# Part of the adaLN modulation of a two-block transformer: matmuls per k-tile replaced by VectorE sums and one matmul over the partitions

## The chip, the cores and the metric

The kernel runs on one core of one Trainium2 chip. The engines of a core are TensorE (PE in the profile, PEld for its weight loads), VectorE (DVE), ScalarE (ACT), GpSimd (POOL) and SyncE (SP, which here issues DMAs). The metric is the time of one execution in microseconds of the device; lower is better.

## What is computed

Two blocks in a row act on 256 tokens of width 1024 (`x`) and on 256 context tokens (`ctx`). All arrays are fp32. The change lies in the first block, which has two layers, each a half feed-forward, an attention mixer, and another half feed-forward; every one of these is wrapped in a modulated norm and a gated residual. The modulation of layer i is a matrix-vector product:

```python
def adaln(cond, w, b):
    m = jax.nn.silu(cond) @ w + b
    return m.reshape(m.shape[:-1] + (N_MOD, D_MODEL))   # 9 x 1024

def modulated_norm(h, g, m, k):
    return rmsnorm(h, g) * (1.0 + m[..., k + 1, :]) + m[..., k, :]

def gated_residual(h, y, g, m, k, weight):
    return h + weight * m[..., k + 2, :] * rmsnorm(y, g)

# layer i:   m = adaln(c, ada_w[i], ada_b[i]);  mc = adaln(c_ctx, ada_w[i], ada_b[i])
#   half_ffn with m rows 0, 1, 2;  mixer with rows 3, 4, 5;  half_ffn with rows 6, 7, 8
```

`ada_w[i]` is 1024 x 9216 (37.7 MB), and there are only two conditions, `c` and `c_ctx`. The feed-forward is `(silu(gate) * up) @ w_out` with 2816 inner columns. The second block (a hybrid layer, twice) is not touched.

## The kernel before

Activations are kept transposed, features on the partitions and the 512 tokens (256 and 256) along the free axis, as eight tiles of 128 features. Every large product is done with three matmuls (`mm3`, lines 78 to 80): weights and activations are each split into a high and a low part, and high x high, low x high and high x low are added up in PSUM. The split of a weight tile is a cast on ScalarE (`wh`, line 60) and a subtraction on VectorE (`wl`, line 61), out of `raw` tiles which SP loads (line 52, three buffers); there are four buffers each of `wh` and `wl`.

A feed-forward (`ffn`) goes through 22 pairs of gate and up columns in three passes of 6, 8 and 8. In each iteration it prepares four weight tiles, runs 24 matmuls for each, takes silu of the gate on ScalarE (line 317), multiplies by up on VectorE (line 319) and splits the product (lines 323 and 324); after each pass `wout` multiplies by the output weights. PSUM gives four banks to gate and up.

The modulation is computed as filler. `ada_w[i]` is cut into 18 blocks of 512 columns, and these into groups of four blocks (`groups`). `adaln` returns a list of functions for a group: loads of 128x512 tiles `adaw` (line 156), eight steps, and a finish. A step takes the four tiles of one k-tile and multiplies each by the 32 columns of `cst` that begin with the two conditions of that k-tile; the four matmuls lie side by side in column strips of the array (line 164), and eight steps add up in one PSUM bank `psada`. The finish copies the bank (line 170), transposes it in four matmuls (line 175) and adds the bias into `mT` (line 182). `set_fill` takes such a list and a number of places; `place`, called after each column pair of `ffn`, each output pair of `wout` and twice in each quarter of an attention head, runs as many functions as keep the list evenly spread. A feed-forward has 22 + 8 = 30 places, the attention `da` 64. A scheduler behind the program orders each engine's instructions by the order of the program and its own estimate of when they can start; on the chip each engine then takes its queue in that order.

Group (i, g) is computed here: (0, 0) before the first feed-forward; (0, 1) and (0, 2) in the first feed-forward, whose `Join` at the end needs them; (0, 3), (1, 0) and (1, 1) in `da`; (0, 4), (1, 2) and (1, 3) partly in steep stretches between stages and partly in the next feed-forward; (1, 4) in the second attention. The small buffers are shared by tags: `adaw` has eight (tag W), and the tag P (four buffers) holds the probabilities of attention and the sums at a feed-forward's end.

Of the kernel before, what the change touches and what calls it, by code (L numbers as in the profile page):

```python
# [6 lines left out]
AF = mybir.ActivationFunctionType  # L7
ALU = mybir.AluOpType
# [4 lines left out]
KC = 8  # L13
# [12 lines left out]
SBUF_TAGS = ({"y": 10, "t": 4, "P": 4, "W": 8},  # L26
             {"d": 10, "e": 7, "m": 7, "t": 1, "th": 2, "E": 3, "br": 4, "mg": 3, "z": 2})
SBUF_OF = {}
for _t, _n in (("y", "y q qh ql kh kl v"), ("W", "adaw sAB sC gPT"), ("t", "q0 k0 sg g adasb vT trot osq o ksq qsq lr lp vr crow csil"), ("P", "P0 P1 PT P aAB aC"),
               ("d", "kz iq kR sc csq ck dq kd vd dPT ya"), ("e", "sbq sbk sbv sbvt yb"), ("m", "mlu mlth mlv wt hn yc"),  # L30
               ("th", "th tho uk"), ("E", "rl dE"), ("br", "bh bl"), ("mg", "mg"), ("z", "z")):
    SBUF_OF.update({n: _t for n in _n.split()})
# [11 lines left out]
class Block:  # L44
# [5 lines left out]
    def load(self, src, nk, cols):  # L50
        raw = self.rawp.tile([128, 8, 256], F32, name="raw", tag="raw")
        self.nc.sync.dma_start(raw[:, 0:nk, 0:cols], src.rearrange("(k p) c -> p k c", p=128))
        return raw
# [87 lines left out]
    def adaln(self, i, blocks, tiles="adaw", ahead=2):  # L141

        nc = self.nc
        nj, b0 = len(blocks), blocks[0]
        gap = blocks[1] - b0
        nm = 4 // nj
        steps = KC // nm
        st = {}

        def load(n):  # L150
            st[n] = []
            for k in range(n * nm, n * nm + nm):
                src = self.I['ada_w'][i, k * 128:(k + 1) * 128, :].rearrange("p (b c) -> p b c", c=512)
                for j in range(nj):
                    w = self.sp.tile([128, 512], F32, name="adas", tag="slot") if tiles == "slot" else self.t2("adaw")
                    nc.sync.dma_start(w, src[:, b0 + gap * j, :])
                    st[n].append(w)

        def step(n):
            if n == 0:  # L160
                st['ps'] = self.pst("psada")
            for q, w in enumerate(st[n]):
                k = n * nm + q // nj
                mm = nc.tensor.matmul(st['ps'][32 * q:32 * q + 32, :], lhsT=self.cst[:, 2 * k:2 * k + 32], rhs=w,
                                      start=n == 0, stop=n == steps - 1, tile_position=(0, 32 * q))
                self.tc.keep_in_program_order(mm)

        def take():
            st['sb'] = self.t2("adasb")
            nc.vector.tensor_copy(st['sb'], st['ps'])  # L170

        def finish():
            pt = self.pst("psadt")
            for q in range(4):
                nc.tensor.transpose(pt[:, q * 128:(q + 1) * 128], st['sb'][:, q * 128:(q + 1) * 128], self.ident)
            g = gap * (nj - 1) + 1
            dst = self.mT[i][:, b0 * 4:(b0 + g) * 4, :].rearrange("p (g q) r -> p q g r", q=4)[:, :, 0:g:gap, :]
            b = self.adab[:, 72 * i + b0 * 4:72 * i + (b0 + g) * 4].rearrange("p (g q) -> p q g", q=4)[:, :, 0:g:gap]
            b = b.unsqueeze(3).to_broadcast([128, 4, nj, 2])
            src = pt.rearrange("p (q m j r) -> p m q j r", q=4, m=nm, r=32)  # L180
            for m in range(nm):
                nc.vector.tensor_tensor(dst, src[:, m, :, :, 0:2], dst if m else b, ALU.add)

        def part(n):
            if n >= 0:
                step(n)
            for k in range(ahead) if n < 0 else (n + ahead,):
                if k < steps:
                    load(k)

        return [lambda n=n: part(n) for n in range(-1, steps - 1)] + [lambda: (step(steps - 1), take()), finish]

    def gtab(self, i, kind, k, out=None, cs=slice(0, 8)):

        nc = self.nc
        t = self.gp.tile([128, 8, 2], F32, name="gt", tag="gt") if out is None else out
        if kind == 'pre':
            j, gi, add, mul = k + 1, {0: 0, 3: 2, 6: 4}[k], 1.0, 1.0
        else:
            j, gi, add, mul = k + 2, {0: 1, 3: 3, 6: 5}[k], 0.0, (1.0 if k == 3 else 0.5)  # L200
        g0, n = (i * 6 + gi) * 8, cs.stop - cs.start
        g = self.ng[:, g0 + cs.start:g0 + cs.stop].unsqueeze(2).to_broadcast([128, n, 2])
        nc.vector.tensor_scalar(t[:, cs, :], self.mT[i][:, j * 8 + cs.start:j * 8 + cs.stop, :], add, mul, ALU.add, ALU.mult)
        nc.vector.tensor_tensor(t[:, cs, :], t[:, cs, :], g, ALU.mult)
        return t
# [1083 lines left out]
    def first_block(self):  # L1289
        nc, I, both = self.nc, self.I, (0, 1)  # L1290
        groups = [range(4 * g, min(4 * g + 4, 18)) for g in range(5)]
        fill = lambda *gs: sum([self.adaln(i, groups[g], ahead=1) for i, g in gs], [])

        us, steps = [], self.adaln(0, (0, 2), "slot", 4)
        us.extend(self.ffn_units(0, 0, 0))

        def begin():
            steps.pop(0)()
            return steps

        R = self.load_tokens(begin)
        for f in steps:
            f()
        self.new_x()
        G = self.gp.tile([128, 8, 2], F32, name="gt", tag="gt")

        def part(cs):
            self.gtab(0, 'pre', 0, G, cs)
            for c in range(cs.start, cs.stop):
                for hf in both:  # L1310
                    s, B = HALF[hf], self.mT[0][:, c, hf:hf + 1]
                    t = self.tp.tile([128, 256], F32, name="t", tag="t", bufs=4)
                    nc.vector.scalar_tensor_tensor(t, self.h[hf][c], G[:, c, hf:hf + 1], R[:, s], ALU.mult, ALU.mult)
                    nc.scalar.activation(self.xh[c][:, s], t, AF.Identity, bias=B)  # L1314
                    if hf:
                        self.low(self.xl[c][:, s], t, B, self.xh[c][:, s])
                    else:
                        nc.vector.scalar_tensor_tensor(self.xl[c][:, s], t, B, self.xh[c][:, s].bitcast(F32), ALU.add, ALU.subtract)

        def steep(i, g):  # L1320

            fl = fill((i, g))
            self.ramp = fl[0:4]
            return fl[4:]

        mid = [us] + self.adaln(0, (1, 3), "slot", 4) + [lambda: part(slice(4, 8))]
        part(slice(0, 4))
        self.ffn(0, 0, both, Join(self, (0, 0), (0, 3)), fill((0, 1), (0, 2)), AF.Exp, mid)
        self.dumph('h1_0')
        self.set_fill(fill((0, 3), (1, 0), (1, 1)), 64)  # L1330
        rest = steep(0, 4)
        self.da(Join(self, (0, 3), (0, 6)))
        self.dump('ya_0', self.y)
        last, rest = rest, steep(1, 2)
        self.ffn(0, 1, both, Join(self, (0, 6), (1, 0)), last)
        self.dumph('h3_0')
        last, rest = rest, steep(1, 3)
        self.ffn(1, 0, both, Join(self, (1, 0), (1, 3)), last, AF.Exp)
        self.set_fill(rest, 10)
        self.edge = self.adaln(1, groups[4], "slot", 2)  # L1340
        self.ga(Join(self, (1, 3), (1, 6)))
        rest, self.edge = self.edge, []
        self.ffn(1, 1, (0,), Join(self, (1, 6), None), rest)
        self.dumph('h3_1')
# [267 lines left out]
```

## Time and profile before

| | |
|---|---|
| runs | 2558.23, 2559.24, 2564.14 us; median 2559.24 |
| profiled execution | 2557.98 us, span of its instructions 2556.3 us |
[...]
| busy share of the span | PE 96%, DVE 56%, ACT 41%, POOL 16% |
| first feed-forward, attention heads, second feed-forward | about 64 to 380, 448 to 712 and 800 to 1120 us of the span |

The span runs from the first to the last instruction. An engine is busy when it executes; waits, and instructions that only issue a DMA, are not counted. A busy PE can still be a slow one, since matmuls overlap and their ends are modelled: the distance of the starts tells the rate. A number of the form "[1.75 <-ACT PT L602]" in a timeline says that the engine was idle for 1.75 us until ScalarE had written PT at line 602.

### The profile page before, as it was taken

To read this page: it belongs to the slowest core of one execution; us is meant where nothing else is said; L and a number is where in the kernel's file an instruction comes from. 1 tells how busy PE (TensorE), PEld (TensorE's weight loads), DVE (VectorE), ACT (ScalarE), POOL (GpSimd) and SP (SyncE) were. 2 spreads that over 40 slices of the span, in tenths; PEclk is the share of its full clock that TensorE was granted. 3 is DMA by queue.
4 is the path that set the end of the run, shared out by engine and by line. 5 is a ranking of instruction groups with operands and counts; after the bars stand their busy time and mean duration, and the time that the engine had idled before them with its cause. 6 is when DMAs were issued, how large, how long until landed. Compare 5 with 4: busy or idle time off the path is not lost. (4 is left out here: it accounts for less than half of the span.)

```text
span 2556.3 us, 37984 instructions
## 1 busy us (share of the span) xinstructions
PE 2447.3 (96%) x15131; PEld 2073.1 (81%) x15131; DVE 1434.3 (56%) x2478; ACT 1035.8 (41%) x1734; POOL 405.9 (16%) x427
## 2 busy tenths in 40 slices
PE   7999999999999999999999999999979999889998
PEld 3777778666678888878788888789968999779998
DVE  4333338666665333375333377666786766676655
ACT  3222225554453222253221255644545544446443
POOL 1000006221051000061000074310240010201010
PEclk9999999999999999999999999999989999999999
DMA  8453532444532322333422344456733456534464
GB/s 287 147 166 119 161 99 85 133 147 154 163 115 84 113 88 96 99 123 125 139 93 92 106 132 132 138 165 198 212 91 109 123 157 186 150 103 129 141 190 132
DMA packets 321789, 346.56 MB, mean 136 GB/s; under 512 B 23906, under 2 KB 282568, under 8 KB 321612
## 3 DMA queue, kind: packets, MB, share of 16 engines
q1 hardware_dynamic: 320706, 343.35, 42.4%
q8 instruction: 119, 1.95, 0.3%
q10 hardware_dynamic: 906, 0.78, 0.1%
q14 instruction: 58, 0.48, 0.1%
HBM read 343.04 MB, written 1.05 MB: 135 GB/s over the span
## 5 line engine op out<-in xcount | busy, mean ns | idle before, releaser
L60 ACT CAST wh<-raw 128x1024 fp32r<-128x1024 f32 (+2 forms) x534 | 528.2, 999 | 1109.1 <-PE psg L79 544.8
L61 DVE TENSOR_TENSOR wl<-raw,wh 128x1024 fp32r<-128x1024 f32 (+2 forms) x534 | 639.8, 1204 | 553.9 <-ACT wh L60 540.8
L79 PE MATMUL psg<-xl,wh 128*128 128x512 f32 (+1 forms) x1472 | 521.2, 355 | 3.3 <-POOL xl L1287 3.3
L78 PE MATMUL psg<-xh,wh 128*128 128x512 f32 (+1 forms) x1472 | 521.4, 356 | 2.9 <-ACT xh L1314 2.3
L80 PE MATMUL psg<-xh,wl 128*128 128x512 f32 (+1 forms) x1472 | 519.1, 353 | 0.0
L78 PE MATMUL psp<-xh,wh 128*128 128x256 f32 x1248 | 354.6, 285 | 13.0 <-ACT xh L855 3.6
L80 PE MATMUL psp<-xh,wl 128*128 128x256 f32 x1248 | 351.8, 282 | 3.3 <-DVE wl L61 3.3
L79 PE MATMUL psp<-xl,wh 128*128 128x256 f32 x1248 | 352.7, 283 | 0.6 <-POOL xl L856 0.6
L78 PEld LDWEIGHTS psg<-xh,wh 128*128 128x128 f32 x1472 | 276.3, 188 | 58.9 <-ACT wh L60 12.6
L79 PEld LDWEIGHTS psg<-xl,wh 128*128 128x128 f32 x1472 | 276.8, 188 | 53.0 <-issue 7.9
L80 PEld LDWEIGHTS psg<-xh,wl 128*128 128x128 f32 x1472 | 276.6, 188 | 39.7 <-issue 0.8
L79 PE MATMUL psy<-gl,wh 128*128 128x512 f32 (+1 forms) x800 | 271.9, 340 | 2.8 <-DVE gl L324 2.7
L78 PE MATMUL psy<-gh,wh 128*128 128x512 f32 (+1 forms) x800 | 273.5, 342 | 0.0
L80 PE MATMUL psy<-gh,wl 128*128 128x512 f32 (+1 forms) x800 | 271.8, 340 | 0.0
L78 PEld LDWEIGHTS psp<-xh,wh 128*128 128x128 f32 x1248 | 237.1, 190 | 22.3 <-issue 5.5
L80 PEld LDWEIGHTS psp<-xh,wl 128*128 128x128 f32 x1248 | 238.0, 191 | 5.1 <-DVE wl L61 4.1
L79 PEld LDWEIGHTS psp<-xl,wh 128*128 128x128 f32 x1248 | 237.9, 191 | 2.8 <-POOL xl L856 1.2
L243 POOL TENSOR_TENSOR acc<-acc,sq 128x256 f32<-128x256 f32 x70 | 57.0, 816 | 1095.3 <-ACT acc L237 1089.7
L319 DVE TENSOR_TENSOR g<-sg,psg 128x512 f32<-128x512 f32 (+1 forms) x88 | 54.7, 621 | 220.2 <-PE psg L80 220.2
L78 PEld LDWEIGHTS psy<-gh,wh 128*128 128x128 f32 x800 | 151.2, 189 | 23.5 <-ACT wh L60 5.0
L79 PEld LDWEIGHTS psy<-gl,wh 128*128 128x128 f32 x800 | 151.5, 189 | 20.2 <-DVE gl L324 3.4
L80 PEld LDWEIGHTS psy<-gh,wl 128*128 128x128 f32 x800 | 151.2, 189 | 18.7 <-issue 1.7
(465 smaller groups left out, 3594.4 us busy)
## 6 DMA issues: line engine op xcount, KB each, us to landing
raw<-in_ffn_w_in SPq DMA_DIRECT2D x88, 1024.0 KB
raw<-in_w_in SPq DMA_DIRECT2D x70, 1024.0 KB
adaw<-in_ada_w SPq DMA_DIRECT2D x240, 256.0 KB
raw<-in_ffn_w_out SPq DMA_DIRECT2D x32, 1024.0 KB
adas<-in_ada_w SPq DMA_DIRECT2D x48, 256.0 KB
raw<-in_ffn_w_out SPq DMA_DIRECT2D x16, 768.0 KB
raw<-in_da_w_in SPq DMA_DIRECT2D x12, 1024.0 KB
raw<-in_w_branch SPq DMA_DIRECT2D x24, 512.0 KB
```

Of the source, the lines that this page charges most:

```text
L60: a = nc.scalar.copy(wh[:, 0:nk, :], r)
L61: b = nc.vector.tensor_sub(wl[:, 0:nk, :], r, wh[:, 0:nk, :].bitcast(F32))
L78: mm(ps, lhsT=wh[:, k, :], rhs=xh, start=first, stop=False)
L79: mm(ps, lhsT=wh[:, k, :], rhs=xl, start=False, stop=False)
L80: mm(ps, lhsT=wl[:, k, :], rhs=xh, start=False, stop=last)
L243: b = (eng or nc.vector).tensor_tensor(acc, acc, sq, ALU.add)
L319: nc.vector.tensor_mul(g[:, 0:width], sg[:, 0:width], pu[:, 0:width])
```

## The change

Five groups, (0, 1), (0, 2), (0, 3), (1, 0) and (1, 1), are computed by a new function, `adaln_sums`. It takes half a group, two blocks, at a time. For each of eight k-tiles it multiplies the two 128x512 tiles by each of the two conditions, whose value for a row of weights is one number per partition, and adds the four products into four tiles `asum` in SBUF: for the first k-tile a scaled copy on ScalarE, for the other seven `scalar_tensor_tensor` on VectorE. Then four matmuls with 32 columns of ones, side by side in the array, add the four tiles up over the partitions into one PSUM bank; ScalarE copies the bank, four matmuls transpose it, and one VectorE instruction adds the bias. A half group is a list of 11 functions: two loads, eight adds (each also loads the tiles of two k-tiles ahead), the total, and the finish.

The groups are placed anew as well: (0, 1), (0, 2) and (0, 3) in the first feed-forward, none in `da`, and (1, 0) and (1, 1) in the second feed-forward, behind the two functions left of (0, 4). The four `asum` tiles share the tag P.

```diff
@@ -26,7 +26,7 @@
 SBUF_TAGS = ({"y": 10, "t": 4, "P": 4, "W": 8},
              {"d": 10, "e": 7, "m": 7, "t": 1, "th": 2, "E": 3, "br": 4, "mg": 3, "z": 2})
 SBUF_OF = {}
-for _t, _n in (("y", "y q qh ql kh kl v"), ("W", "adaw sAB sC gPT"), ("t", "q0 k0 sg g adasb vT trot osq o ksq qsq lr lp vr crow csil"), ("P", "P0 P1 PT P aAB aC"),
+for _t, _n in (("y", "y q qh ql kh kl v"), ("W", "adaw sAB sC gPT"), ("t", "q0 k0 sg g adasb vT trot osq o ksq qsq lr lp vr crow csil"), ("P", "P0 P1 PT P aAB aC asum"),
                ("d", "kz iq kR sc csq ck dq kd vd dPT ya"), ("e", "sbq sbk sbv sbvt yb"), ("m", "mlu mlth mlv wt hn yc"),
                ("th", "th tho uk"), ("E", "rl dE"), ("br", "bh bl"), ("mg", "mg"), ("z", "z")):
     SBUF_OF.update({n: _t for n in _n.split()})
@@ -189,6 +189,53 @@
                     load(k)
 
         return [lambda n=n: part(n) for n in range(-1, steps - 1)] + [lambda: (step(steps - 1), take()), finish]
+
+    def adaln_sums(self, i, blocks):
+
+
+        nc, out = self.nc, []
+        for b0 in blocks[::2]:
+            st = {}
+
+            def load(k, b0=b0, st=st):
+                st[k] = []
+                for b in (b0, b0 + 1):
+                    w = self.t2("adaw")
+                    nc.sync.dma_start(w, self.I['ada_w'][i, k * 128:(k + 1) * 128, b * 512:b * 512 + 512])
+                    st[k].append(w)
+
+            def add(k, load=load, st=st):
+                if k == 0:
+                    st['a'] = [self.t2("asum") for _ in range(4)]
+                for n, a in enumerate(st['a']):
+                    w, s = st[k][n // 2], self.cst[:, 2 * k + n % 2:2 * k + n % 2 + 1]
+                    if k == 0:
+                        nc.scalar.activation(a, w, AF.Identity, scale=s)
+                    else:
+                        nc.vector.scalar_tensor_tensor(a, w, s, a, ALU.mult, ALU.add)
+                if k + 2 < KC:
+                    load(k + 2)
+
+            def total(st=st):
+                ps = self.pst("psada")
+                for n, a in enumerate(st['a']):
+                    mm = nc.tensor.matmul(ps[32 * n:32 * n + 32, :], lhsT=self.ones[:, 0:32], rhs=a, tile_position=(0, 32 * n))
+                    self.tc.keep_in_program_order(mm)
+                st['sb'] = self.t2("adasb")
+                nc.scalar.copy(st['sb'], ps)
+
+            def finish(b0=b0, st=st):
+                pt = self.pst("psadt")
+                for q in range(4):
+                    nc.tensor.transpose(pt[:, q * 128:(q + 1) * 128], st['sb'][:, q * 128:(q + 1) * 128], self.ident)
+                v = lambda a: a.rearrange("p (g q) r -> p q g r", q=4)
+                b = self.adab[:, 72 * i + b0 * 4:72 * i + b0 * 4 + 8].rearrange("p (g q) -> p q g", q=4)
+                nc.vector.tensor_tensor(v(self.mT[i][:, b0 * 4:b0 * 4 + 8, :]),
+                                        pt.rearrange("p (q j r z) -> p q j r z", q=4, j=2, z=32)[:, :, :, :, 0],
+                                        b.unsqueeze(3).to_broadcast([128, 4, 2, 2]), ALU.add)
+
+            out += [lambda load=load: (load(0), load(1))] + [lambda k=k, add=add: add(k) for k in range(KC)] + [total, finish]
+        return out
 
     def gtab(self, i, kind, k, out=None, cs=slice(0, 8)):
 
@@ -1290,6 +1337,7 @@
         nc, I, both = self.nc, self.I, (0, 1)
         groups = [range(4 * g, min(4 * g + 4, 18)) for g in range(5)]
         fill = lambda *gs: sum([self.adaln(i, groups[g], ahead=1) for i, g in gs], [])
+        sums = lambda *gs: sum([self.adaln_sums(i, groups[g]) for i, g in gs], [])
 
         us, steps = [], self.adaln(0, (0, 2), "slot", 4)
         us.extend(self.ffn_units(0, 0, 0))
@@ -1325,14 +1373,14 @@
 
         mid = [us] + self.adaln(0, (1, 3), "slot", 4) + [lambda: part(slice(4, 8))]
         part(slice(0, 4))
-        self.ffn(0, 0, both, Join(self, (0, 0), (0, 3)), fill((0, 1), (0, 2)), AF.Exp, mid)
+        self.ffn(0, 0, both, Join(self, (0, 0), (0, 3)), sums((0, 1), (0, 2), (0, 3)), AF.Exp, mid)
         self.dumph('h1_0')
-        self.set_fill(fill((0, 3), (1, 0), (1, 1)), 64)
+        self.set_fill((), 64)
         rest = steep(0, 4)
         self.da(Join(self, (0, 3), (0, 6)))
         self.dump('ya_0', self.y)
         last, rest = rest, steep(1, 2)
-        self.ffn(0, 1, both, Join(self, (0, 6), (1, 0)), last)
+        self.ffn(0, 1, both, Join(self, (0, 6), (1, 0)), last + sums((1, 0), (1, 1)))
         self.dumph('h3_0')
         last, rest = rest, steep(1, 3)
         self.ffn(1, 0, both, Join(self, (1, 0), (1, 3)), last, AF.Exp)
```

## Rows read from the trace of the kernel before

**Rows 1.** The page: busy time by engine, share of the span, instructions.
```profile
PE 2447.3 (96%) x15131; PEld 2073.1 (81%) x15131; DVE 1434.3 (56%) x2478; ACT 1035.8 (41%) x1734; POOL 405.9 (16%) x427
```

**Rows 2.** Three stretches: length, busy time (count) by engine, granted clock, DMA.
```profile
64.00:380.00 316.00, 316.00 (x1441) 246.71 (x1440) 111.21 (x140) 75.40 (x92) 0.79 (x2) 1.00 0.43 140
448.00:712.00 264.00, 249.93 (x1406) 173.91 (x1405) 167.52 (x367) 122.52 (x270) 42.01 (x49) 0.99 0.45 144
800.00:1120.00 320.00, 317.32 (x1432) 263.75 (x1431) 121.61 (x152) 86.50 (x120) 28.97 (x29) 0.99 0.30 98
```

**Rows 3.** Two of them, adaLN matmuls (line 164) alone: PE and weight load.
```profile
64.00:380.00 316.00, 17.04 (x128) 2.52 (x128) 1.00 0.43 140
448.00:712.00 264.00, 27.65 (x192) 4.04 (x192) 0.99 0.45 144
```

**Rows 4.** Timeline of PE around one adaLN step: start, duration, line, tiles.
```profile
64.80 0.39 PE L78 MATMUL psg<-xh,wh 128*128 128x512 f32 x1
...
66.62 0.39 PE L80 MATMUL psg<-xh,wl 128*128 128x512 f32 x1
66.94 1.06 PE L164 MATMUL psada<-adaw,cst 128*32 128x512 f32 x8
...
68.27 0.39 PE L79 MATMUL psg<-xl,wh 128*128 128x512 f32 x1
```

**Rows 5.** Timeline of PE around one set of adaLN transposes.
```profile
369.59 0.39 PE L80 MATMUL psg<-xh,wl 128*128 128x512 f32 x1
369.82 0.60 PE L175 MATMUL psadt<-ident,adasb 128*128 128x128 f32 x4
...
370.49 0.39 PE L79 MATMUL psg<-xl,wh 128*128 128x512 f32 x1
```

**Rows 6.** Four attention heads, L164 alone; the transposes inside the last two.
```profile
499.45:530.38 30.93, 4.26 (x32) 0.63 (x32) 1.00 0.71 225
595.94:626.91 30.97, 4.26 (x32) 0.63 (x32) 1.00 0.48 150
530.38:559.36 28.98, 2.13 (x16) 0.32 (x16) 1.00 0.22 70
626.91:656.32 29.41, 2.13 (x16) 0.32 (x16) 1.00 0.51 165
...
541.34 0.60 PE L175 MATMUL psadt<-ident,adasb 128*128 128x128 f32 x4
...
628.76 0.66 PE L175 MATMUL psadt<-ident,adasb 128*128 128x128 f32 x4
```

**Rows 7.** PE in attention where its clock falls, and the stretch behind.
```profile
568.14 2.07 PE L607 MATMUL pso<-v,PT 128*128 128x128 f32 x8 [1.75 <-ACT PT L602]
...
568.20:573.80 5.60, 5.60 (x17) 4.79 (x18) 1.90 (x5) 3.39 (x8) 2.02 (x3) 0.50 0.02 7
```

**Rows 8.** Timeline of DVE in the first feed-forward, one tile pair.
```profile
207.97 0.69 DVE L319 TENSOR_TENSOR g<-sg,psg 128x512 f32<-128x512 f32 x1 [3.42 <-PE psg L80]
...
214.20 1.23 DVE L61 TENSOR_TENSOR wl<-raw,wh 128x1024 fp32r<-128x1024 f32 x1 [3.35 <-ACT wh L60]
218.85 0.69 DVE L319 TENSOR_TENSOR g<-sg,psg 128x512 f32<-128x512 f32 x1 [3.42 <-PE psg L80]
```

**Rows 9.** Groups by line and form: prices of DVE and ACT work.
```profile
L1151 DVE SCALAR_TENSOR_TENSOR mlu<-mlth,mlu 128x512 f32<-128x512 f32 x8 | 7.3, 907 | 0.4 <-ACT mlth L1150 0.4
...
L1002 DVE SCALAR_TENSOR_TENSOR z<-yb,z 128x512 f32<-128x512 f32 x4 | 2.8, 692 | 0.1
...
L622 ACT ACTIVATE oh<-psot,sub 128x512 fp32r<-128x512 f32 x8 | 5.5, 683 | 7.6 <-PE psot L619 7.6
```

**Rows 10.** SP's own queue in the first feed-forward: waits, total, times, longest.
```profile
SPq L52 <- DVE wl L61: 154.8, 18, 16.8
SPq L156 <- PE psada L164: 119.5, 14, 20.1
```

**Rows 11.** The adaLN sums' copy: who waited for it (us, times).
```profile
  PEld psadt L175: 2.4, 2
```

## The prediction

> **What bounds the kernel now.** I read the page first, for which engine is short of time: TensorE (PE) is busy in 96% of the span, VectorE (DVE) in 56%, ScalarE (ACT) in 41% [rows 1]. Then the stretches by stage, because an average hides where DVE has room. In the first feed-forward PE is busy for all of 316.00 us while DVE works 111.21 and ACT 75.40; in the second it is 317.32 of 320 us against 121.61 and 86.50. In the attention heads PE works 249.93 of 264 us, so 14.07 us are waits there, and DVE works 167.52 [rows 2]. The reader is to see that DVE has some two thirds of both feed-forwards free, and that any instruction taken off PE there moves everything behind it.
>
> Then the adaLN matmuls alone: 128 records in the first feed-forward and 192 in the heads [rows 3]. The timeline draws one step as 8 records [rows 4], four matmuls of two passes each, so these are 16 and 24 steps: two groups of eight and three groups of eight, as the code has them.
>
> **Price of a step on PE.** From 64.80 to 66.62 us lie eight ordinary starts, 0.2275 us each. With a step between them the second ordinary matmul behind 66.62 starts at 68.27, 1.65 us later, where two starts would take 0.455: a step costs 1.20 us [rows 4]. A set of four transposes by the same reckoning: 370.49 - 369.59 = 0.90, less 0.455, is 0.45 us [rows 5].
>
> **First feed-forward, PE.** It loses 16 steps and two sets: 16 x 1.20 + 2 x 0.45 = 20.1 us. It gains six half groups (three groups now, two halves each), each one quartet with ones over the partitions, of the shape of a step (128x32 by 128x512), and one set: 6 x (1.20 + 0.45) = 9.9. Net -10.2 us.
>
> **Second feed-forward, PE.** Four half groups arrive: 4 x 1.65 = +6.6 us.
>
> **Attention, PE.** 24 steps and three sets leave: 24 x 1.20 + 3 x 0.45 = 30.2 us at most; nothing at least, if PE would have waited in their place. The nearest rows are the heads themselves. Two heads with four steps take 30.93 and 30.97 us, two with two steps and one set take 28.98 and 29.41 [rows 6]. The difference of the means, 1.76 us, stands against 2 x 1.20 - 0.45 = 1.95: nine tenths of a step's price is paid in time. At that rate 27 us come off; as the steps go altogether, the 14 us of waits should grow a little, and I take 25.
>
> [...]
>
> **DVE and ACT.** A half group is seven accumulating passes of four 128x512 instructions, 28. No row has this one; the same operation with all operands in SBUF takes 0.69 us, and the dearest of that shape 0.91 [rows 9]. I take 0.69, since the slower one belongs to another stage. First feed-forward: 6 x 28 x 0.69 = 116 us on top of 111.21, 72% of 316 (at 0.91: 153, 84%). Second: 4 x 28 x 0.69 = 77 on 121.61, 62%. I cost them at nothing; the cover is PE's own stream. In one tile pair of 10.88 us (207.97 to 218.85) DVE waits 3.35 + 3.42 = 6.8 us [rows 8], and the steps are spread over 30 places, one each tile pair or output pair, so one place brings 168 / 30 = 5.6 instructions, 3.9 us (5.1 at the dear price). It fits, and what they push back is not at once needed: a freed weight buffer or PSUM bank is used again a tile pair or more later. Without that cover each microsecond of excess would come on the end once per place. ACT's first pass of a half, four scaled copies at 0.68 [rows 9], and the copy out of PSUM are 6 x 3.4 = 20 us on 75.40: nothing.
>
> **Waits that come new.** Each half ends in a quartet that waits for the last four DVE adds, and transposes that wait for a copy. Behind them on PE stand the feed-forward's own matmuls. Today such transposes wait 2.4 us in two cases [rows 11]; with ten halves for five groups, and the quartet's wait beside it, I add 2 us (0 to 12, if all ten waited 1.2).
>
> **DMA.** The same 256 KB tiles are loaded, 160 of them in all, on SP's queue; 32 more in the first feed-forward and 64 in the second, 8.4 and 16.8 MB, where DMA is 43% and 30% busy [rows 2]. Hidden. Four groups are ready well ahead of their readers, and (1, 1) has the whole next block.
>
> **Sum.** -10.2 + 6.6 - 25 + 2 = -26.6 us. The profiled execution took 2557.98 us (span 2556.3 and 1.7 around it), so 2531. That execution lies 1.3 us below the median of the runs; I leave the forecast on its side. Bounds: all 30.2 in attention, no new wait and the fall of rows 7 gone, -10.2 + 6.6 - 30.2 - 2.8 = -36.6, 2521; nothing in attention, 2556. What a measurement here can tell from no change is 0.3%, 7.7 us.
>
> **Rivals.**
> 1. Attention does not give the time back: its heads are chains from scores to maximum, exponential, transposes and product, and steps filled their gaps. For it: 14 us of waits. Against it: rows 6. Half of the 30 gives -10.2 + 6.6 - 15 + 2 = -16.6, 2541 us; nothing gives 2556.
> 2. On the other side: loads hold up DVE. An accumulating add is queued on DVE in a fixed order; if its tile has not landed, it holds back the weight split (line 61) and the PSUM reads behind it, and PE stops. Today a late tile holds only PE's step. SP's queue already stands 119.5 us for adaLN buffers and 154.8 for weight buffers [rows 10], so a tile can queue behind a weight load that itself waits for DVE. Against it: two to four steps of tiles fit in the eight buffers, and DVE has 2.9 us to spare per place. The gain of 26.6 is gone at 26.6 / 60 places = 0.44 us of stop per place; at 1 us the time is 2591. [...]
> 3. The clock: one fall of 2.8 us in each of eight heads, 22 us, against today's one stretch in rows 7. That gives 2531 + 22 = 2553. The granted mean of 0.99 in the heads [rows 2] speaks against it.
>
> **How the numbers follow.** The forecast, 2531 with 2521 to 2538 as its own range: 0.67. Rival 1 at half 0.14, at nothing 0.04; rival 2 0.08; rival 3 0.07. Faster by over 0.3%: the forecast, rival 1 at half, and 0.01 of rival 3 with fewer falls, 0.82. Within 0.3%: rival 1 at nothing, the other 0.06 of rival 3, and 0.01 of rival 2 about its threshold, 0.11. Slower: the other 0.07 of rival 2. The range reaches from 2519 (the bound, and 2 us for the heads' new order) to 2549, past rival 1 at half and six of rival 3's eight falls; it leaves out rival 2, rival 1 at nothing and most of rival 3, 0.18.
>
> **What would show it.** Adds of 128x512 on DVE near 0.69 us, 280 of them; DVE near 72% and PE still at 100% in the first feed-forward, which ends some 10 us earlier; heads of 26 to 27 us; the second feed-forward 6 to 9 us longer. I am wrong if PE waits in the feed-forwards for line 60 or 61 or for adaLN tiles, if the heads keep 29 us with PE waiting, or if the granted clock in the heads falls well under 0.99.

## The result and the profile after

The changed kernel takes 2539.14 us (median of four runs, 2537.06 to 2541.03) against 2561.18 us of the kernel before beside it: a ratio of 0.9915, with a 95% interval of 0.9899 to 0.993. The profiled execution took 2537.06 us, span 2535.3 us. The granted TensorE clock, mean over the span, was 0.985 of full speed in both kernels' profiled executions. The forecast was 2531 us in a range of 2519 to 2549.

The page of the changed kernel, busy time by engine, answers to [rows 1]:

```profile
PE 2419.7 (95%) x14911; PEld 2070.8 (82%) x14911; DVE 1611.6 (64%) x2758; ACT 1064.3 (42%) x1784; POOL 410.4 (16%) x427
```

VectorE has 177 us more to do, TensorE 28 us less. Where the time went is read between three marks that both traces have: the first row sum (`psst` from `aAB`) at the end of the first feed-forward, the start of `warm`, a small ScalarE instruction behind attention's last head, and the same row sum at the end of the second feed-forward. "Attention" below is the stretch from the first mark to the second. The stretches between them, first of the kernel before, then of the changed one (length, then busy time of PE, PEld, DVE, ACT and POOL, granted clock, DMA share, GB/s):

```profile
418.20:714.10 295.90, 277.87 (x1581) 199.04 (x1580) 193.09 (x426) 140.59 (x305) 59.07 (x66) 0.97 0.43 136
714.10:1126.20 412.10, 403.62 (x2017) 338.58 (x2016) 186.71 (x266) 136.32 (x224) 75.29 (x74) 0.99 0.32 103
1126.20:2556.30 1430.10, 1365.59 (x9670) 1229.29 (x9668) 888.03 (x1525) 641.25 (x1023) 233.02 (x244) 0.98 0.45 138
```

```profile
409.20:680.90 271.70, 254.64 (x1388) 195.61 (x1389) 187.54 (x421) 138.04 (x305) 60.66 (x66) 0.98 0.17 56
680.90:1101.30 420.40, 410.32 (x2053) 338.82 (x2053) 260.38 (x382) 148.43 (x244) 76.50 (x74) 0.99 0.43 140
1101.30:2535.30 1434.00, 1364.10 (x9670) 1229.58 (x9668) 887.59 (x1525) 641.38 (x1023) 234.59 (x244) 0.98 0.45 138
```

The first mark comes 9.0 us earlier (418.2 to 409.2), attention is 24.2 us shorter, the second feed-forward 8.3 us longer, and 3.9 us are lost behind it, where both kernels run the same 9670 matmuls. In attention PE's busy time falls by 23.2 us and its waits stay: 18.0 before, 17.1 after. In the second feed-forward 6.7 us of the 8.3 are work.

The first feed-forward itself and four heads of the changed kernel, which answer to [rows 2, 6]; the columns are the same:

```profile
64.00:373.00 309.00, 308.13 (x1387) 249.22 (x1386) 216.10 (x305) 91.29 (x115) 0.00 (x0) 1.00 0.53 172
```

```profile
486.29:512.31 26.02, 26.01 (x134) 19.16 (x135) 18.89 (x43) 13.48 (x30) 2.89 (x3) 1.00 0.28 86
512.31:539.99 27.68, 26.61 (x141) 19.67 (x141) 18.93 (x43) 13.94 (x32) 3.64 (x5) 1.00 0.06 18
571.31:598.99 27.68, 26.52 (x141) 19.67 (x141) 18.94 (x43) 13.51 (x30) 2.84 (x3) 1.00 0.06 19
598.99:626.58 27.59, 25.82 (x137) 19.08 (x138) 18.19 (x41) 12.71 (x28) 2.84 (x3) 1.00 0.29 97
```

PE is still full in the feed-forward while DVE is at 70%. The two heads that had four steps went from 30.93 and 30.97 to 26.02 and 27.68 us, the two with two steps and a set of transposes from 28.98 and 29.41 to 27.68 and 27.59.

The new instructions by tile `asum` (min, median and max in ns, then the first and last start):

```profile
L215 DVE SCALAR_TENSOR_TENSOR asum<-adaw,cst,asum x280: 739/747/1232, 53.6 to 997.7; 128x512 f32<-128x512 f32 x140
L222 PE MATMUL psada<-asum,ones x80: 592/604/617, 100.4 to 1048.1; 128*32 128x512 f32 x80
```

One add is 0.747 us long, but the next instruction starts before it ends: eleven in a row from 103.71 us take 7.37 us, 0.67 each.

### The profile page after: what moved, and what is told of

Its sections match the earlier page's. It is cut to its first block, busy times and chain, and to the rows that moved or that the text cites. A ratio compares the mean times of both kernels' runs of the same rounds, so it can differ in the third digit from the quotient of the medians.

```text
span 2535.3 us, 37930 instructions
## 1 busy us (share of the span) xinstructions
PE 2419.7 (95%) x14911; PEld 2070.8 (82%) x14911; DVE 1611.6 (64%) x2758; ACT 1064.3 (42%) x1784; POOL 410.4 (16%) x427
## 4 chain that ended last, share of the span: by engine, by line
PE 67%; DVE 12%; issue 11%; ACT 4%; POOL 4%; DMA 3%; SPq 0%; ACTq 0%; DVEq 0%; POOLq 0%
PE psg L79 11%; PE psg L78 11%; PE psg L80 11%; PE psy L78 5%; PE psy L79 5%; PE psy L80 5%; DVE wl L61 4%; PE psp L79 2%; PE psp L78 2%; PE psp L80 2%; PE psada L164 2%; DMA raw<-in_w_in 2%; ACT wh L60 1%; POOL acc L290 1%; PE pso L654 1%
## 5 line engine op out<-in xcount | busy, mean ns | idle before, releaser
L215 DVE SCALAR_TENSOR_TENSOR asum<-adaw,cst,asum 128x512 f32<-128x512 f32 x280 | 194.1, 756 | 1.3 <-ACT asum L213 1.1
L78 PEld LDWEIGHTS psy<-gh,wh 128*128 128x128 f32 x800 | 151.1, 189 | 22.7 <-ACT wh L60 4.2
```

Of the source, the lines that this page charges most:

```text
L78: mm(ps, lhsT=wh[:, k, :], rhs=xh, start=first, stop=False)
L215: nc.vector.scalar_tensor_tensor(a, w, s, a, ALU.mult, ALU.add)
```

## The experiments

The theory was that PE's stream sets the time in all three stages: a step is paid wherever it stands, and VectorE's work is free as long as it stays under PE's. The table gives the marks of each profiled execution, in us; a stage that an experiment meant to change is bold. Ratios are to the kernel before on the same chip, whose median was 2559 to 2561 us each time.

| kernel | to mark 1 | attention | second feed-forward | behind | median of runs |
|---|---|---|---|---|---|
| before | 418.2 | 295.9 | 412.1 | 1430.1 | 2561.18 |
| changed | 409.2 | 271.7 | 420.4 | 1434.0 | 2539.14 |
| groups moved only | **428.4** | 273.1 | **434.1** | 1439.7 | 2572.56 |
| sums in attention | **403.8** | **283.6** | 420.4 | 1430.0 | 2541.99 |
| half more adds | **418.1** | 278.3 | **417.2** | 1427.8 | 2544.45 |
| adds doubled | **462.8** | 276.2 | **418.8** | 1429.3 | 2588.56 |
| totals twice | **427.6** | 271.6 | **427.1** | 1432.3 | 2559.10 |
| steps back in attention | 410.7 | **296.0** | 420.1 | 1431.3 | 2560.07 |
| all sums | 409.1 | 276.1 | **418.9** | **1434.0** | 2540.58 |
| one set per group | **408.3** | 273.2 | **415.3** | 1431.5 | 2529.30 |
| changed, again | 409.4 | 276.4 | 418.9 | 1431.5 | 2536.19 |

**The groups moved, the steps kept.**

```diff
-self.ffn(0, 0, ..., sums((0, 1), (0, 2), (0, 3)), AF.Exp, mid)
+self.ffn(0, 0, ..., fill((0, 1), (0, 2), (0, 3)), AF.Exp, mid)
-self.ffn(0, 1, ..., last + sums((1, 0), (1, 1)))
+self.ffn(0, 1, ..., last + fill((1, 0), (1, 1)))
```

> The groups are placed as in the changed kernel (three in the first feed-forward, two in the second, none in attention), but computed as before, by steps of four matmuls per k-tile on PE. Theory (a step costs 1.20 us of PE wherever PE is full): against the kernel before, the first feed-forward gets 8 steps and one set of transposes more (+10 us), the second 16 steps and two sets (+20), attention loses 24 us: 2559 + 6 = 2565 us, about 26 above the changed kernel. Rival (it is leaving attention that pays, and how the sums are made does not matter): 2535 to 2545 us.

Measured: 2572.56 us, 1.0061 of the kernel before (1.0044 to 1.0078). The first feed-forward grew by 10.2 us and the second by 22.0, as 8 and 16 steps with their transposes should (10 and 20); attention is about as short as in the changed kernel (273.1 against 271.7). Moving alone therefore loses: what attention saves the feed-forwards pay, and the gain comes from summing on VectorE. The total lies above the forecast by 7.6 us; the profiled execution, the slowest of its four at 2577.07 us, took 9.6 us more than the kernel before behind the marks, in code that is the same.

**Steps put back into attention, without loads and without a use.** The steps multiply tiles that lie in SBUF anyway.

```diff
-self.set_fill((), 64)
+self.set_fill(sum([self.adaln(0, groups[3], "hc", 1) for _ in range(3)], []), 64)
 # adaln, tiles == "hc": st[n] = list(self.hc), no DMA; the transposed bank is copied to a scratch tile
```

> As the changed kernel, but attention gets the 24 steps and three sets of transposes of the kernel before back, on tiles that are in SBUF anyway, with no loads and no result that is used. Theory (attention became shorter by PE's time): +24 to +27 us, 2563 to 2566. Rival (attention became shorter since 96 loads left SP's queue and the DMA rings): 2539 to 2545 us.

Measured: 2560.07 us, 1.0008 of the kernel before (0.9995 to 1.0021). Attention of this kernel:

```profile
410.70:706.70 296.00, 277.58 (x1583) 198.63 (x1584) 193.42 (x427) 140.09 (x306) 59.05 (x66) 0.98 0.16 51
```

It takes 296.0 us with DMA at 0.16, where the kernel before took 295.9 at 0.43. The loads had no part in it; the 24 steps, with their three sets of transposes, are the difference. The total is 20.9 us above the changed kernel's 2539.14, where 24 to 27 were expected; the intervals of the two ratios, 3 to 4 us to either side each, do not tell the two apart.

**Group (0, 3) summed in attention.**

```diff
-self.ffn(0, 0, ..., sums((0, 1), (0, 2), (0, 3)), AF.Exp, mid)
+self.ffn(0, 0, ..., sums((0, 1), (0, 2)), AF.Exp, mid)
-self.set_fill((), 64)
+self.set_fill(self.adaln_sums(0, groups[3], True), 32)   # asum in buffers of the slot pool
```

> As the changed kernel, but group (0, 3) is summed during the first heads of attention (its sums held in other buffers) and not in the first feed-forward. Theory (the place matters, since VectorE has room in a feed-forward and little in attention): the first feed-forward is 3 us shorter, four heads get 42 us more of VectorE on some 70 of 105, so they become bound by it: 2547 to 2565 us. Rival (VectorE at two thirds in attention has room enough): 2539 us, within 3 us of the changed kernel.

Measured: 2541.99 us, 0.9947 (0.9929 to 0.9965). By the total the rival would have it. The stages say otherwise: the first feed-forward is 5.4 us shorter than in the changed kernel, attention about 9 longer than in the executions without steps there (271.6 to 278.3), where two halves on PE explain 3.3. In the first heads:

```profile
430.00:560.00 130.00, 119.94 (x634) 90.26 (x633) 117.80 (x237) 68.90 (x147) 36.81 (x38) 0.97 0.31 96
```

DVE is at 91% there. PE's waits for DVE in this window (`o`, `dg` and `P`) come to 4.2 us, against 1.3 in as long a window behind the changed kernel's first mark. So adds cost time in attention, as the theory has it, but that VectorE bounds these heads is only in part shown: PE is busy for 92% of the same window. The price, 9 us, lies below the 11 to 29 that 2547 to 2565 us stand for, and the shorter first feed-forward hid most of it.

**Totals and transposes done twice.**

```diff
-... + [total, finish]
+... + [total, finish, total, finish]
```

> As the changed kernel, but each half group's total over the partitions and its four transposes are done twice. Theory (1.65 us of PE for each of ten halves, none hidden): +16.5 us, 2555 to 2556. Rival (they fall into gaps, or their waits are what costs): 2539 to 2543 us, or well above 2560 if each waits.

Measured: 2559.10 us, 1.0008 (0.9994 to 1.0022). The second feed-forward grew by 6.7 us for four halves, 1.68 each, where 1.65 was reckoned. The first grew by 18.4 instead of 9.9. The timeline of PE shows the largest part of the excess:

```profile
75.32 0.80 PE L80 MATMUL psg<-xh,wl 128*128 128x512 f32 x1 [3.26 <-DVE wl L61]
...
76.77 0.63 PE L80 MATMUL psg<-xh,wl 128*128 128x512 f32 x1
```

Early in this feed-forward DVE is busy without a pause, and its queue has another order: four more adds stand ahead of the next four weight splits, the first of which starts at 74.05 us, where the changed kernel starts it at 66.69. PE waits 3.26 us for a split; the changed kernel waits 0.9 us at this place. Behind the wait a matmul takes 0.63 us in place of 0.39, and the starts lie 0.43 us apart in place of 0.23, as in the stretch at 0.50 of [rows 7]; so a part of the stop is paid a second time. Against the changed kernel the first of the 22 products `g` (line 366 there) starts 2.6 us later, for a reason that was not looked for, the third 9.2 us later, and the last 18.4: what comes between the third and the last is the price of the totals, 9.2 where 9.9 was reckoned.

**Half as many adds again, and all adds doubled.** Second adds have a factor of zero.

```diff
 nc.vector.scalar_tensor_tensor(a, w, s, a, ALU.mult, ALU.add)
+if n < 2:                      # doubled: for all n
+    nc.vector.scalar_tensor_tensor(a, w, self.cst[:, 40:41], a, ALU.mult, ALU.add)
```

> As the changed kernel, but two of the four adds of each k-tile are followed by a second one with a factor of zero: half as much again on VectorE. At the 0.75 us that an add takes, the first feed-forward gets 63 us more, 279 of 309. Theory (VectorE costs nothing while it stays under PE's stream): 2539 to 2543 us. Rival (VectorE's queue holds PE up long before it is full): 2550 us or more.

> As the changed kernel, but every add is followed by a second one with a factor of zero. The first feed-forward needs 342 us of VectorE against 309 of PE, the second some 290 of 325. Theory: the first becomes bound by VectorE and grows by 33 us or a little more, the second does not: 2572 to 2582 us. Rival (VectorE does not reach the path at all): 2539 to 2543 us.

Measured: 2544.45 us (0.9945, 0.993 to 0.996) and 2588.56 us (1.0117, 1.0103 to 1.0131). The first lies 1.5 us above the theory's range and well below the rival's 2550; the second lies 6.6 us above the theory's. The first feed-forward with half more, its head and the rest of it:

```profile
64.00:90.00 26.00, 20.63 (x83) 16.32 (x82) 26.00 (x39) 7.57 (x9) 0.00 (x0) 0.87 0.70 222
90.00:382.00 292.00, 292.00 (x1317) 236.20 (x1316) 246.38 (x355) 85.33 (x108) 0.00 (x0) 1.00 0.51 163
```

The time to the first mark grew by 8.9 us, and it is lost by the end of this head (2.5 us of it already at the first product `g`): DVE is busy for all of its 26 us, PE waits 4.6 us for a weight split, and the clock falls to 0.87. The share alone is not the reason, for in the changed kernel DVE is busy for 25.4 of the same 26 us. In the 292 us behind it DVE is at 84%, and PE does not wait. With doubled adds, the first feed-forward and the middle of the second:

```profile
64.00:427.00 363.00, 326.54 (x1395) 258.93 (x1394) 326.26 (x475) 93.07 (x119) 0.00 (x0) 0.95 0.47 147
805.00:1085.00 280.00, 279.65 (x1287) 229.27 (x1286) 249.16 (x362) 81.24 (x105) 5.64 (x6) 1.00 0.46 149
```

The waits of PE in the doubled first feed-forward (total, times, longest):

```profile
PE psg L80 <- DVE wl L61: 25.9, 5, 8.6
PE psy L80 <- DVE wl L61: 7.9, 4, 2.7
```

The first feed-forward now has 326 us of DVE work where PE took 309 (342 were reckoned, at 0.75 for an add instead of the 0.67 at which adds start in a row). The time to the first mark grew by 53.6 us, more than the 33 that the theory put on DVE's time alone: 36.5 us of waits, and 0.05 of the clock over 363 us, 18 us. In the second feed-forward DVE is at 89% over 280 us, PE waits 0.3 us of them at full clock, and the stage is no longer than in the changed kernel. So VectorE's work was free up to 89% of a stretch. It cost time where the stage has not enough of it for all adds, and at the head of the first feed-forward, where adds stand ahead of the weight splits.

**All groups by sums.** The steps that filled the ends of two feed-forwards and the second attention are gone too.

```diff
-last, rest = rest, steep(1, 2)
+last = rest
-last, rest = rest, steep(1, 3)
-self.ffn(1, 0, both, Join(...), last, AF.Exp)
-self.set_fill(rest, 10)
+self.ffn(1, 0, both, Join(...), sums((1, 2), (1, 3)), AF.Exp)
+self.set_fill((), 10)
```

> As the changed kernel, but groups (1, 2) and (1, 3) too are made by sums, in the third feed-forward; their steps at the ends of the second and third feed-forward (three each), in the third feed-forward (five) and in the second attention (five) are gone. Theory (PE's time): the third feed-forward 0, the second attention -6.4 us, the ends of the feed-forwards a little less: 2530 to 2534 us. [...]

Measured: 2540.58 us, 0.993 (0.9918 to 0.9943): 6.6 us above the theory's range. Two stretches between instructions that both kernels have (from mark 3 to the next such row sum, and from `warm` to `warm` around the second attention), first of this kernel, then of the changed one:

```profile
1104.10:1129.80 25.70, 21.72 (x139) 19.68 (x138) 23.43 (x47) 16.95 (x34) 14.48 (x16) 0.80 0.24 72
...
1449.40:1623.30 173.90, 158.72 (x990) 141.27 (x989) 118.24 (x231) 93.65 (x194) 76.17 (x77) 0.94 0.24 79
```

```profile
1101.30:1126.00 24.70, 24.70 (x164) 17.75 (x162) 22.95 (x47) 15.72 (x32) 14.52 (x16) 1.00 0.47 151
...
1444.10:1615.60 171.50, 164.31 (x1037) 136.93 (x1036) 120.61 (x232) 93.83 (x195) 77.13 (x77) 0.98 0.40 129
```

PE is busy for 3.0 and 5.6 us less, in stretches that are 1.0 and 2.4 us longer (the ten other executions take 24.6 to 25.0 and 169.9 to 172.9 us for them). Instead it waits, 4.0 us for 0.0 and 15.2 for 7.2, and the granted clock falls from 1.00 to 0.80 and from 0.98 to 0.94. There the steps stood in gaps, and with them the clock was higher. The third feed-forward between the two stretches, forecast at 0, is 1.9 us longer.

**One set of transposes per group.** The total of a half uses a pattern of 16 columns of ones and 16 of zeros, the second half the other way round, and both add up in one bank.

```diff
-lhsT=self.ones[:, 0:32], rhs=a, tile_position=(0, 32 * n))
+lhsT=self.pat[:, h, :], rhs=a, start=h == 0, stop=h == 1, tile_position=(0, 32 * n))
-[total, finish]
+([total, finish] if h else [total])
```

> As the changed kernel, but both halves of a group add their totals into one bank (the second half into rows 16 to 31 of each strip, by a pattern of ones and zeros), so that a group needs one copy and one set of transposes as before the change. Theory (0.45 us of PE for a set, and a little for its wait): five sets less, -2.3 to -3.5 us against the changed kernel. Rival (sets fall into gaps): within 1 us of it.

> The changed kernel itself once more, as the measure of the run beside it: 2536 to 2542 us. A profile of a second execution also tells how much the stages behind the change move by themselves; the theory that the last 4 us lost there are chance expects another figure in them, between -5 and +5 us of the kernel before; the rival (the change itself costs them) expects +4 again.

Measured side by side: 2529.30 us (0.9872, 0.9852 to 0.9891) and 2536.19 us (0.9902, 0.9885 to 0.9919). This is the fastest version run, though the two intervals just meet; the difference of 6.9 us is about twice the 3.5 that was the most forecast. Against the execution beside it the first feed-forward is 1.1 us shorter (three sets, 1.35) and the second 3.6; of these two sets are 0.9, and a wait of 2.2 us of the changed kernel for a product at the head of `wout` (`gl`) is not in its trace. The other profiles of the changed kernel and of its variants with more adds or totals all have that wait. These two stages make 4.7 us; attention's 3.2 of difference lies before the second head, at a granted clock of 0.93 against 0.87, and is of the kind that the same kernel shows between two executions, below. Behind the marks the second execution of the changed kernel took 1431.5 us, 1.4 above the kernel before and not 3.9: so that loss was mostly chance, as far as two executions tell.

## Why the prediction was right

**First feed-forward.** Forecast -10.2 and a share of the new waits, measured -9.0. One stop of 0.9 us is what PE had there.

**Second feed-forward.** Forecast +6.6 and the rest of the waits. Measured +8.3 in the profile and +6.8 in the second execution; doubling the totals gave 1.68 us a half.

**Attention.** That the steps give their time back when they leave was right, as the steps put back show, and the waits did not grow (18.0 to 17.1 us). The size was somewhat off: 25 us were taken off, and this profile shows 24.2, but the eight executions without steps lie between 271.6 and 278.3 us, on average 274.6, 21.3 below the kernel before. Split at the transposes that close the first head and the seventh (`psot`), with the granted clock of the first part:

| kernel | to the end of the first head | clock | next six heads | rest |
|---|---|---|---|---|
| before | 81.2 | 0.94 | 189.9 | 24.8 |
| steps back in attention | 79.8 | 0.96 | 190.7 | 25.5 |
| changed; totals twice | 77.1 | 0.96 | 169.8; 169.7 | 24.8 |
| groups moved only; one set per group | 78.6 | 0.93 | 169.6; 169.7 | 24.8; 24.9 |
| all sums; adds doubled; changed, again | 81.7; 81.7; 81.8 | 0.87 | 169.6; 169.6; 169.8 | 24.8; 24.9; 24.8 |
| half more adds | 82.1 | 0.88 | 171.3 | 24.9 |

What differs among the kernels without steps is nearly all in the first part, and goes with its clock. Compared at about the same clock, taking the steps out gave 2.6 to 2.7 us there (three steps), 20 to 21 in the six heads (19 steps, two sets) and 0 to 0.7 in the rest (two steps, one set): 22.7 to 24.4 in all. The term of the working that was mis-sized is the rate of nine tenths of 1.20 us, 1.08 a step, for all 24 steps: in the six heads a step gave 1.01 (20.1 less 0.90 for two sets, over 19), and the last two steps with their set next to nothing. Rows 6 compared four heads and drew too much from two pairs. That 25 came as near as it did is in part luck of the execution profiled, which had the higher clock; the average of 21.3 holds four executions that had the lower one. The lower clock of the first part came in four of eight executions without steps and in neither of the two with them, and in one of two executions of the very same program, so whether it has to do with the steps is open.

**VectorE.** An add is 0.747 us long, between the two prices named, but in a row they start 0.67 us apart, close to the 0.69 taken. 70% in the first feed-forward was forecast as 72. That this is free holds but for one stop of 0.9 us, and the runs with more adds put no price on up to 89% of a stretch.

**Sum.** By the averages -9.0 - 21.3 + 8 or so + 1 to 2 behind the marks makes -20 to -21, against -26.6 forecast and -22.0 in the medians. The median of before lies above its profiled run and that of after too, so 3.2 of the 8 us between 2531 and 2539.14 are the choice of the run that the sum stood on: from the median 2561.18 the same sum gives 2534.6. The rest is the sum itself, attention's size above all.

**Rivals.** The chain of the heads (rival 1) had a small part: the last two steps and their set stood in time that stayed. Loads holding DVE (rival 2) did not happen: in both feed-forwards of the changed kernel DVE waits for no load. The order of its queue does matter (in the changed kernel's profile DVE starts its 2694 instructions in the order of the program), as the stop of 3.26 us behind doubled totals shows, but by the adds' own work. The clock (rival 3) did not fall in every head, as that rival has it: the six heads, taken as one stretch, ran at 0.98 to 1.00 (in the changed kernel at 0.99, five of them at 1.00 and one at 0.95). The 2.8 us which that rival and the bounds take for a fall can only be estimated, as half of the 5.60 us that [rows 7] show at 0.50; no run shows the price of a single fall. What the runs show is 4.7 us between the first part at 0.87 and at 0.96, in the two executions of the changed kernel. What the profile of the changed kernel alone does not show is that over the whole of attention four of the eight executions without steps ran at 0.95 or 0.96, against 0.97 and 0.98 with steps; that cost them 4.4 to 6.6 us, all by the end of the fourth head. In the kernel with all sums the clock also fell at other places, and there the gain was gone.

## What to carry to other kernels

Where one engine is full and another has room in the same stage, moving a reduction over was worth the full engine's time here (9.0 us in the first feed-forward, where 10.2 were reckoned); count the stage, not the span. The helper was nearly full here (89% over 280 us) at no cost, in a stage that has time for all its work; look at the order of its queue at the head of the stage, since the stops of a full TensorE cost clock beside the wait (with doubled adds 18 us, at a granted 0.95, beside 36.5 of waits). Before a filler is removed, look whether its stretch is full (the six heads gave back 1.01 us a step) or waiting (with all sums the stretch behind mark 3 gave nothing: it became 1.0 us longer, and its clock fell from 1.00 to 0.80). Small instructions that come once per half group, here copies and transposes, are the next thing to merge.

## What was not expected of the hardware

The same program takes different times over the same instructions. From the first mark to the end of the first head, the changed kernel's two executions:

```profile
409.20:486.29 77.09, 69.03 (x419) 57.40 (x419) 61.09 (x140) 43.02 (x89) 30.28 (x33) 0.96 0.17 54
```

```profile
409.40:491.20 81.80, 74.35 (x419) 62.85 (x419) 61.07 (x140) 42.98 (x89) 30.23 (x33) 0.87 0.16 51
```

77.1 and 81.8 us for the same 419 matmuls: the granted clock was 0.96 in one and 0.87 in the other, since it came back later (0.86 in the first 24.4 us and 1.00 in the rest, against 0.78 in the first 25.6 us and 0.92 in the rest). That is the whole difference of the two executions' attention (271.7 and 276.4 us). The stretch behind the marks lies between 1427.8 and 1439.7 us in kernels whose code is the same there; why was not tried. A gain of a few microseconds can therefore not be read from one pair of profiles, and the stage that holds a joint, where one part of the program hands over to the next and TensorE waits, is the worst place to read it.
